# Hybrid mixer block on one core: a second Sx buffer, a third decay-matrix buffer, and two groups of instructions issued later

## The chip, the core and the metric

One core of a Trainium2 chip runs the whole program. The time is device microseconds from launch to end, median of several runs. The engines are PE (matrix products), DVE (vector), ACT (activations, casts and copies), POOL (here a DMA queue and some fills) and SP (a DMA queue).

## What is computed

One layer over 512 latent tokens of 1024 channels and 256 context tokens: a modulated RMSNorm, three mixers that run on the same input (a gated DeltaNet in both directions, a short gated convolution, a Fourier mixing), gates that merge them, an output projection, and a SwiGLU. All matrices are fp32. The change lies in the DeltaNet, which works on chunks of 64 tokens, four heads and two directions:

```python
g = jnp.cumsum(g, axis=-1)
decay = jnp.exp(jnp.where(lower, g[..., :, None] - g[..., None, :], -jnp.inf))
a = jnp.where(strict, jnp.einsum("bhnid,bhnjd->bhnij", kb, k) * decay, 0.0)
t_inv = lax.linalg.triangular_solve(a + eye, ...)      # unit lower triangular
u = t_inv @ (v * beta[..., None])
w = t_inv @ (kb * jnp.exp(g)[..., None])
attn = jnp.einsum("bhnid,bhnjd->bhnij", q, k) * decay
...
v_new = u_i - jnp.einsum("bhcd,bhde->bhce", w_i, s)    # scan over the chunks
o_i = jnp.einsum("bhcd,bhde->bhce", qg_i, s) + jnp.einsum("bhij,bhje->bhie", attn_i, v_new)
s = s * jnp.exp(gl_i)[..., None, None] + jnp.einsum("bhcd,bhce->bhde", kd_i, v_new)
```

## The kernel before, in words

**Main GEMMs.** `gemm_fm` multiplies a slice of 256 columns of a weight by the normalised input. Weights are fetched in halves of 512 KB by SP (`wf`, three buffers), split into a high part (an ACT cast, L143) and a low part (a DVE subtraction, L144), two buffers each, and multiplied three times (L255 to L257). A product with the 512 latent tokens (LAT) goes to a bank of pool `g` (three of them), one with the 256 context tokens (CTX) to a bank of pool `d` (four). In program order a half does first LAT, then CTX, with 24 instructions each.

**Order.** The program is written in Tile: each instruction has a priority (the places are, from the first to the last: setup, tri, sub, scan, prep, main), and within a place an earlier line goes first. A scheduler walks through the program with modelled times and gives each engine what is ready, by priority; on the chip each engine then runs its list in that fixed order, with semaphores. A buffer is asked for where the program makes the tile, and a tile with `bufs=1` waits until all readers of the one before it are done.

**DeltaNet.** Behind the key GEMM, at place `tri`, L404 to L440 work out the log decays G from the 16 columns of beta and alpha; L444 transposes them, DVE cumulates them (L447 to L466, giving `Gr`; scratch in `gtmp`, which has the tag `Sx`), and POOL stores `Gr` and a mirrored copy `Gn` to DRAM (L476 to L479). L480 to L502 turn them into columns: two transposes into a `d` bank (L481, L482), `Gc`, its exponentials `eGn` and `eG`, a product with ones into a second `d` bank (L494), the exponentials `eGl` and `ekd`, and the sigmoid of beta (L502). Then, at place `main`, come two value GEMMs (L504, LAT and CTX), each followed by its convolution and SiLU (`pairs`), and two query GEMMs.

For each of three batches of four chunk pairs (context, then two of latent tokens): `decay_gram` loads rows of decays from DRAM into `E` (L564, POOL), subtracts them from `Gc` (L565), takes exponentials, multiplies by Gram products (L578, in the single bank `t`) and scales; `substitute` inverts the 32x32 diagonal blocks by 60 dependent DVE steps (L611, L612) and stores them transposed to DRAM (L614); `inverse` loads them back (L620, `Sx`), transposes on DVE (L622), copies them to the diagonal of `TBD` (L625, four ACT copies), and makes the off-diagonal block: 64 products of 32x32 in bank `t` (L631; the trace's x64), two ACT copies to `Z` (L634), 64 products with `Sx` (L638), two ACT copies to `TBD` (L641). `scan(b)` does four dependent steps on `TBD` (L716). For the latent batches it first makes two masked decay matrices `ET` (L549 to L555: POOL load, two DVE steps, one exponential) at place `main`; each is read by two steps (L682). The order of calls is gram 0, gram 1, substitute both, inverse 0, scan 0, inverse 1, gram 2, substitute 2, scan 1, inverse 2, scan 2. Main GEMMs of later stages (L758 on) run on PE beside all this wherever they are ready.

Of the kernel before, what the change touches and what calls it, by code (L numbers as in the profile page):

```python
# [9 lines left out]
F32 = mybir.dt.float32  # L10
# [64 lines left out]
def body(tc, I, out):  # L75
    nc = tc.nc
    V, A, T, SY, GP = nc.vector, nc.scalar, nc.tensor, nc.sync, nc.gpsimd
    es = ExitStack()
    with es:
# [10 lines left out]
        pD = dstack.enter_context(tc.tile_pool(name="pD", bufs=1))  # L90
# [14 lines left out]
        def tbank(name="t"):  # L105
            return pst.tile([128, 512], F32, name=name, tag="t")

        def dbank(name="d"):
            return psd.tile([128, 512], F32, name=name, tag="d")
# [8 lines left out]
        def cst(name, rows=slice(None)):  # L118
            a, b = COFF[name]
            return cp[rows, a:b]  # L120
# [15 lines left out]
        def load_w(src, n=256):  # L136
            with prio("prep"):
                w = stg.tile([128, 4, 256], F32, name="wf", tag="wf", bufs=3)
                SY.dma_start(out=w[:, :, :n], in_=src)
            return w  # L140
# [5 lines left out]
        def prep_w(w, n=256, scale=None, dst=None):  # L146
            with prio("prep"):
                if dst is None:
                    wh = stg.tile([128, 4, 256], F32R, name="wh", tag="wh", bufs=2)
                    wl = stg.tile([128, 4, 256], F32R, name="wl", tag="wl", bufs=2)  # L150
                else:
                    wh, wl = dst
                if scale is not None:
                    V.tensor_tensor(out=w, in0=w, in1=scale, op=ALU.mult)  # L154
                split(w[:, :, :n], wh[:, :, :n], wl[:, :, :n])
            return wh, wl
# [97 lines left out]
        def mm3(ps, lh, ll, rh, rl, start, stop):  # L254
            T.matmul(ps, lhsT=lh, rhs=rh, start=start, stop=False)  # L255
            T.matmul(ps, lhsT=lh, rhs=rl, start=False, stop=False)  # L256
            T.matmul(ps, lhsT=ll, rhs=rh, start=False, stop=stop)  # L257
# [78 lines left out]
        def gemm_fm(wsrc, targets, n=256, kt=8):  # L336

            nt, mw = max(1, n // 128), min(n, 128)
            ps = {(ti, q): targets[ti][3]() for ti in range(len(targets)) for q in range(nt)}
            for half in range(kt // 4):  # L340
                wh, wl = prep_w(load_w(wsrc[:, 4 * half:4 * half + 4, :], n), n)
                for ti, (rh, rl, nn, _) in enumerate(targets):
                    for q in range(nt):
                        cs = slice(128 * q, 128 * q + mw)
                        for kk in range(4):
                            k = 4 * half + kk
                            mm3(ps[ti, q][0:mw, :nn], wh[:, kk, cs], wl[:, kk, cs], rh(k), rl(k), k == 0, k == kt - 1)
            return [[ps[ti, q] for q in range(nt)] for ti in range(len(targets))]
# [19 lines left out]
        def taps(base, stride, ft):  # L368
            return [cols2[:, base + stride * k + ft:base + stride * k + ft + 1] for k in range(3)]
# [4 lines left out]
        def pairs(dsts, ps, n, row, tp):  # L374

            y = cvt()[:, :n]
            conv3(y, ps[:, :n], tp, row)
            for i, dst in enumerate(dsts):
                sl = slice(256 * i, 256 * i + 256)
                d = dst.rearrange("p (m c j) -> p m c j", m=2, j=64)  # L380
                v = lambda t: t.rearrange("p (m b j) -> p m b j", m=2, j=64)
                A.activation(out=d[:, :, 0::3, :], in_=v(y[:, sl]), func=AF.Silu)
                A.activation(out=d[:, :, 1:3, :], in_=v(y[:, ::-1][:, sl]), func=AF.Silu)
# [19 lines left out]
        with prio("tri"):  # L403
# [38 lines left out]

            pg = dbank()
            T.transpose(pg[0:64, 0:128], G.rearrange("p a m h -> p (a m h)"), ident)  # L444
            gtmp = pD.tile([64, 512], F32, name="gtmp", tag="Sx", bufs=1)
            gr = gtmp[:, 0:128]
            V.tensor_copy(gr, pg[0:64, 0:128])  # L447
            gw = gtmp[:, 128:256]
# [28 lines left out]
            for i in range(2):  # L477
                GP.dma_start(out=Gd[:, 1, :, 32 * i:32 * i + 32].rearrange("u r j -> r u j"), in_=Gr[:, :, 32 - 32 * i:64 - 32 * i])
            GP.dma_start(out=Gdn.rearrange("u r j -> r u j"), in_=Gn)  # L479
            pg = dbank()  # L480
            T.transpose(pg[:, 0:64], Grf, ident[0:64, 0:64])  # L481
            T.transpose(pg[:, 64:128], Gn.rearrange("r u j -> r (u j)"), ident[0:64, 0:64])  # L482
            Gc = col("Gc")
            V.tensor_copy(flat(Gc), pg[:, 0:64])
            eGn = col("eGn")
            A.activation(out=flat(eGn), in_=pg[:, 64:128], func=AF.Exp)
            eG = col("eG")
# [7 lines left out]
            eGl = const.tile([128, 2, 64], F32, name="eGl")  # L495
            A.activation(out=eGl.rearrange("p u c -> p (u c)"), in_=pl[:, 0:128], func=AF.Exp)
            ekd = col("ekd")
# [2 lines left out]
                V.tensor_tensor(out=flat(ekd)[us], in0=pl[us, 64 * u:64 * u + 64], in1=flat(Gc)[us], op=ALU.subtract)  # L500
            A.activation(out=ekd, in_=ekd, func=AF.Exp)
            A.activation(out=bv, in_=bv, func=AF.Sigmoid)  # L502
        for g2 in range(2):
            pl_, pc_ = gemm_fm(win[:, :, 1024 + 256 * g2:1280 + 256 * g2], (LAT, CTX))  # L504
            for q in range(2):
                h = 2 * g2 + q
                tp = taps(0, 12, 8 + h)
                pairs([VT[0][:, h]], pc_[q], 256, 256, tp)
                pairs([VT[1][:, h], VT[2][:, h]], pl_[q], 512, 64, tp)
# [21 lines left out]
        TBD = pD.tile([128, 2, 16, 128], F32, name="TBD", tag="TBD")  # L531
# [14 lines left out]

        def decay_T(b, mm):

            ET = pD.tile([128, 2, 4, 64], F32, name="ET", tag="ET2", bufs=2)  # L549
            for u in range(2):  # L550
                src = Gdn[u].rearrange("(a r) j -> a r j", a=2)[:, 8 * b + 4 * mm:8 * b + 4 * mm + 4, :]
                GP.dma_start(out=ET[64 * u:64 * u + 64].rearrange("p a h j -> p a (h j)"), in_=src.rearrange("a r j -> a (r j)").partition_broadcast(64))
            V.tensor_tensor(out=ET, in0=ET, in1=Gc[:, :, 2 * b + mm, :].unsqueeze(3).broadcast_to([128, 2, 4, 64]), op=ALU.subtract)
            V.tensor_tensor(out=ET, in0=ET, in1=cst("mT").rearrange("p (a j) -> p a j", a=2).unsqueeze(2).broadcast_to([128, 2, 4, 64]), op=ALU.min)
            A.activation(out=ET, in_=ET, func=AF.Exp)  # L555
            return ET

# [58 lines left out]
        def inverse(b):  # L616

            slot, E = b % 2, Es[b]
            Sx = pD.tile([128, 16, 32], F32, name="Sx", tag="Sx", bufs=1)
            SY.dma_start(out=Sx, in_=Lt[b].rearrange("x p c -> p x c"))  # L620
            Sy = E[:, :, 0:32]
            V.transpose(out=Sy, in_=Sx)  # L622
            for q in range(4):
                qs = slice(32 * q, 32 * q + 32)
                A.copy(out=TBD[qs, slot, :, 32 * q:32 * q + 32], in_=Sy[qs])  # L625
            Z = pD.tile([128, 16, 32], F32, name="Z", tag="sh", bufs=1)
            bank = tbank()
            for i in range(16):
                for u in range(2):
                    a0, b0 = 64 * u, 64 * u + 32  # L630
                    T.matmul(bank[a0:a0 + 32, 32 * i:32 * i + 32], lhsT=E[b0:b0 + 32, i, 32:64], rhs=Sy[b0:b0 + 32, i, :],  # L631
                             start=True, stop=True, tile_position=(b0, a0))
            for a0 in (0, 64):
                A.copy(out=Z[a0:a0 + 32].rearrange("p i j -> p (i j)"), in_=bank[a0:a0 + 32])  # L634
            bank = tbank()
            for i in range(16):
                for a0 in (0, 64):
                    T.matmul(bank[a0:a0 + 32, 32 * i:32 * i + 32], lhsT=Sx[a0:a0 + 32, i, :], rhs=Z[a0:a0 + 32, i, :],  # L638
                             start=True, stop=True, tile_position=(a0, a0))
            for a0 in (0, 64):  # L640
                A.activation(out=TBD[a0:a0 + 32, slot, :, a0 + 32:a0 + 64], in_=bank[a0:a0 + 32].rearrange("p (i j) -> p i j", j=32),  # L641
                             func=AF.Copy)
# [11 lines left out]

        def scan_step(s, ET=None):
            b, par, m = s // 4, s % 2, s // 2
# [79 lines left out]
        def scan(b):  # L736
            ETs = [decay_T(b, mm) if b else None for mm in range(2)]
            with prio("scan"):
                for mm in range(2):
                    for par in range(2):  # L740
                        scan_step(4 * b + 2 * mm + par, ETs[mm])

        with prio("tri"):
            decay_gram(0)
            decay_gram(1)
            substitute((0, 1))
            inverse(0)
        scan(0)
        with prio("tri"):
            inverse(1)  # L750
            decay_gram(2)
            substitute((2,))
        scan(1)
        with prio("tri"):
            inverse(2)
# [351 lines left out]
```

## Time and profile before

| | |
|---|---|
| time, median of 3 runs | 975.82 us (973.52, 975.82, 976.12) |
| time of the profiled execution | 972.6 us |
| its span, first to last instruction | 970.8 us |
| PE busy | 953.0 us, 98% of the span |
| weight loads into PE (PEld) | 784.9 us, 81% |
| DVE busy | 544.4 us, 56% |
| ACT busy | 417.9 us, 43% |
| POOL busy | 28.8 us, 3% |
| mean granted PE clock | 0.997 of full speed |

In a timeline each row is a start (us from the start of the span), a duration, the engine, line, operation and the tiles written and read; in brackets the idle time of the engine before it, and what ended that. A row with a count (x64) is that many instructions merged.

### The profile page before, as it was taken

To read this page: it belongs to the slowest core of one execution; us is meant where nothing else is said; L and a number is where in the kernel's file an instruction comes from. 1 tells how busy PE (TensorE), PEld (TensorE's weight loads), DVE (VectorE), ACT (ScalarE), POOL (GpSimd) and SP (SyncE) were. 2 spreads that over 40 slices of the span, in tenths; PEclk is the share of its full clock that TensorE was granted. 3 is DMA by queue.
4 is the path that set the end of the run, shared out by engine and by line. 5 is a ranking of instruction groups with operands and counts; after the bars stand their busy time and mean duration, and the time that the engine had idled before them with its cause. 6 is when DMAs were issued, how large, how long until landed. Compare 5 with 4: busy or idle time off the path is not lost.

```text
span 970.8 us, 14622 instructions
## 1 busy us (share of the span) xinstructions
PE 953.0 (98%) x5964; PEld 784.9 (81%) x5964; DVE 544.4 (56%) x880; ACT 417.9 (43%) x729; POOL 28.8 (3%) x47
## 2 busy tenths in 40 slices
PE   8999999899999999999999999999999999999997
PEld 7587887778788888888878888988888888888885
DVE  3575888369765423788874977333333333434455
ACT  5363884687863334362234346332323232211224
POOL 1002200000000000000000000000000000000000
PEclk9999999999999999999999999999999999999999
DMA  9820542512202232837774352223233333232322
GB/s 336 285 66 4 133 131 83 136 45 55 57 23 65 87 109 69 306 110 270 252 237 158 103 173 62 69 87 105 92 100 95 95 102 89 91 103 89 106 87 87
DMA packets 96836, 115.30 MB, mean 119 GB/s; under 512 B 18124, under 2 KB 84032, under 8 KB 96768
## 3 DMA queue, kind: packets, MB, share of 16 engines
q1 hardware_dynamic: 88192, 109.01, 35.5%
q0 software_dynamic: 1632, 3.44, 1.7%
q10 hardware_dynamic: 6944, 1.91, 0.8%
q8 instruction: 47, 0.77, 0.3%
q14 instruction: 21, 0.17, 0.1%
HBM read 110.58 MB, written 3.77 MB: 118 GB/s over the span
## 4 chain that ended last, share of the span: by engine, by line
PE 45%; DMA 3%; DVE 2%; issue 0%; ACT 0%; DVEq 0%
PE g L257 12%; PE g L256 12%; PE g L255 11%; PE d L257 2%; PE d L256 2%; PE d L255 2%; DMA wf<-in_w_ffn_out_dram 2%; DVE wl L144 1%; PE t L257 1%; PE t L256 1%; PE t L255 1%; DMA wm<-in_w_mod_dram 1%; DMA wf<-in_w_gate_dram 1%; DVE wf L154 1%; PE d L1032 0%
## 5 line engine op out<-in xcount | busy, mean ns | idle before, releaser
L144 DVE TENSOR_TENSOR wl<-wf,wh 128x1024 fp32r<-128x1024 f32 x131 | 160.0, 1222 | 214.4 <-ACT wh L143 213.7
L143 ACT CAST wh<-wf 128x1024 fp32r<-128x1024 f32 x131 | 137.8, 1053 | 299.1 <-PE g L256 161.5
L257 PE MATMUL g<-hh,wl 128*128 128x512 f32 x368 | 146.2, 397 | 0.3 <-DVE wl L144 0.3
L256 PE MATMUL g<-hl,wh 128*128 128x512 f32 x368 | 146.0, 397 | 0.0
L255 PE MATMUL g<-hh,wh 128*128 128x512 f32 x368 | 145.8, 396 | 0.0
L255 PE MATMUL g<-h2h,wh 128*128 128x512 f32 (+1 forms) x352 | 133.6, 380 | 0.0
L257 PE MATMUL g<-h2h,wl 128*128 128x512 f32 (+1 forms) x352 | 133.5, 380 | 0.0
L256 PE MATMUL g<-h2l,wh 128*128 128x512 f32 (+1 forms) x352 | 133.5, 379 | 0.0
L257 PEld LDWEIGHTS g<-hh,wl 128*128 128x128 f32 x368 | 69.6, 189 | 14.3 <-DVE wl L144 0.7
L256 PEld LDWEIGHTS g<-hl,wh 128*128 128x128 f32 x368 | 69.6, 189 | 14.1 <-issue 0.5
L255 PEld LDWEIGHTS g<-hh,wh 128*128 128x128 f32 x368 | 69.5, 189 | 13.6 <-issue 0.2
L256 PEld LDWEIGHTS g<-h2l,wh 128*128 128x128 f32 x352 | 66.2, 188 | 12.6
L255 PEld LDWEIGHTS g<-h2h,wh 128*128 128x128 f32 x352 | 66.2, 188 | 12.5
L257 PEld LDWEIGHTS g<-h2h,wl 128*128 128x128 f32 x352 | 66.1, 188 | 12.4
L154 DVE TENSOR_TENSOR wf<-wf,g2b 128x1024 f32<-128x1024 f32 x22 | 27.0, 1225 | 55.1 <-DMA wf<-in_w_ffn_out_dram 55.0
L830 DVE SCALAR_TENSOR_TENSOR acc<-wm,ct,acc 128x1024 f32<-128x1024 f32 x32 | 41.0, 1282 | 15.5 <-DMA acc<-in_b_mod_dram 7.3
L256 PE MATMUL d<-wl,Ga 128*128 128x512 f32 x72 | 28.0, 390 | 0.0
L257 PE MATMUL d<-wh,Ga 128*128 128x512 f32 x72 | 28.0, 389 | 0.0
L255 PE MATMUL d<-wh,Ga 128*128 128x512 f32 x72 | 28.0, 389 | 0.0
L713 ACT ACTIVATE SJ<-SJ,eGl 128x128 f32<-128x128 f32 x80 | 25.2, 403 | 3.9 <-PE d L701 3.5
L143 ACT CAST Ga<-cvg 128x512 fp32r<-128x512 f32 x18 | 11.1, 619 | 25.4 <-DVE cvg L1078 25.4
L256 PE MATMUL g<-wl,Ga 128*128 128x512 f32 x54 | 21.2, 393 | 0.1
(464 smaller groups left out, 1704.9 us busy)
## 6 DMA issues: line engine op xcount, KB each, us to landing
wm<-in_w_mod_dram SPq DMA_DIRECT2D x48, 512.0 KB, 5.5
wf<-in_w_ffn_in_dram SPq DMA_DIRECT2D x44, 512.0 KB, 3.5
wf<-in_w_in_dram SPq DMA_DIRECT2D x31, 512.0 KB, 3.9
wf<-in_w_gate_dram SPq DMA_DIRECT2D x24, 512.0 KB, 3.7
wf<-in_w_ffn_out_dram SPq DMA_DIRECT2D x22, 512.0 KB, 3.5
wf<-in_w_o_dram SPq DMA_DIRECT2D x8, 512.0 KB, 3.6
xl<-in_x_dram SPq DMA_DIRECT2D x4, 512.0 KB, 5.3
wf<-in_w_sc_out_dram SPq DMA_DIRECT2D x4, 512.0 KB, 3.3
```

The costliest lines, as they stand in the source:

```text
L143: A.copy(out=hi, in_=f)
L144: V.tensor_tensor(out=lo, in0=f, in1=hi.bitcast(F32), op=ALU.subtract)
L154: V.tensor_tensor(out=w, in0=w, in1=scale, op=ALU.mult)
L255: T.matmul(ps, lhsT=lh, rhs=rh, start=start, stop=False)
L256: T.matmul(ps, lhsT=lh, rhs=rl, start=False, stop=False)
L257: T.matmul(ps, lhsT=ll, rhs=rh, start=False, stop=stop)
L713: A.activation(out=S[:, u ^ par, h], in_=S[:, u ^ par, h], func=AF.Copy, scale=eGl[:, u, c_:c_ + 1])
L830: V.scalar_tensor_tensor(out=acc, in0=w, scalar=ct[:, k, 0:1], in1=acc, op0=ALU.mult, op1=ALU.add)
```

## The change

`gtmp` and the `Sx` tiles get two buffers instead of one, `ET` three instead of two. The decay columns become a function that is called behind the first value GEMM, at place `main` instead of `tri`. In `inverse`, the four copies to the diagonal of `TBD` stand behind the two `Z` copies.

```diff
-            gtmp = pD.tile([64, 512], F32, name="gtmp", tag="Sx", bufs=1)
+            gtmp = pD.tile([64, 512], F32, name="gtmp", tag="Sx", bufs=2)
...
             GP.dma_start(out=Gdn.rearrange("u r j -> r u j"), in_=Gn)
+        def decay_columns():
             pg = dbank()
             T.transpose(pg[:, 0:64], Grf, ident[0:64, 0:64])
...
             A.activation(out=bv, in_=bv, func=AF.Sigmoid)
+            return Gc, eGn, eG, eGl, ekd
+
         for g2 in range(2):
             pl_, pc_ = gemm_fm(win[:, :, 1024 + 256 * g2:1280 + 256 * g2], (LAT, CTX))
+            if g2 == 0:
+                Gc, eGn, eG, eGl, ekd = decay_columns()
             for q in range(2):
...
-            ET = pD.tile([128, 2, 4, 64], F32, name="ET", tag="ET2", bufs=2)
+            ET = pD.tile([128, 2, 4, 64], F32, name="ET", tag="ET2", bufs=3)
...
-            Sx = pD.tile([128, 16, 32], F32, name="Sx", tag="Sx", bufs=1)
+            Sx = pD.tile([128, 16, 32], F32, name="Sx", tag="Sx", bufs=2)
             SY.dma_start(out=Sx, in_=Lt[b].rearrange("x p c -> p x c"))
             Sy = E[:, :, 0:32]
             V.transpose(out=Sy, in_=Sx)
-            for q in range(4):
-                qs = slice(32 * q, 32 * q + 32)
-                A.copy(out=TBD[qs, slot, :, 32 * q:32 * q + 32], in_=Sy[qs])
...
             for a0 in (0, 64):
                 A.copy(out=Z[a0:a0 + 32].rearrange("p i j -> p (i j)"), in_=bank[a0:a0 + 32])
+            for q in range(4):
+                qs = slice(32 * q, 32 * q + 32)
+                A.copy(out=TBD[qs, slot, :, 32 * q:32 * q + 32], in_=Sy[qs])
             bank = tbank()
```

## Rows read from the trace of the kernel before

**Rows 1.** The page's head and busy times of the engines.

```profile
span 970.8 us, 14622 instructions
PE 953.0 (98%) x5964; PEld 784.9 (81%) x5964; DVE 544.4 (56%) x880; ACT 417.9 (43%) x729; POOL 28.8 (3%) x47
```

**Rows 2.** Windows: busy time and count by engine, granted clock, DMA share, GB/s.

```profile
84.00:87.00 3.00, 3.00 (x18) 2.27 (x9) 1.40 (x7) 1.53 (x3) 0.00 (x0) 0.50 0.00 0
...
93.00:96.00 3.00, 1.66 (x9) 0.95 (x8) 2.12 (x12) 0.64 (x3) 1.61 (x3) 1.00 0.04 11
...
178.00:204.00 26.00, 22.85 (x490) 18.09 (x490) 8.81 (x16) 21.72 (x42) 2.12 (x4) 1.00 0.29 73
...
700.00:800.00 100.00, 100.00 (x443) 82.82 (x442) 34.30 (x37) 29.36 (x37) 0.00 (x0) 1.00 0.32 100
```

The engines of a window stand in the order PE, PEld, DVE, ACT, POOL.

**Rows 3.** Timeline of PE around the decay columns, and four transposes later.

```profile
92.70 0.39 PE L256 MATMUL g<-hl,wh 128*128 128x512 f32 x1
92.93 0.39 PE L257 MATMUL g<-hh,wl 128*128 128x512 f32 x1
94.15 0.27 PE L481 MATMUL d<-cp,Gr 64*128 64x64 f32 x1 [0.83 <-DVE Gr L465]
...
95.62 0.39 PE L255 MATMUL d<-HC,wh 128*128 128x256 f32 x1
...
101.47 0.40 PE L255 MATMUL g<-hh,wh 128*128 128x512 f32 x1
...
213.45 0.66 PE L664 MATMUL d<-cp,KV 128*128 128x128 f32 x4
```

**Rows 4.** Timelines of ACT and DVE around the decay columns.

```profile
83.76 0.24 ACT L502 ACTIVATE beta<-beta 128x48 f32<-128x48 f32 x1 [2.74 <-DVE beta L424]
...
85.73 0.19 DVE L429 TENSOR_SCALAR smt<-smt 128x48 f32<-128x48 f32 x1 [1.43 <-ACT smt L428]
...
105.15 1.22 DVE L565 TENSOR_TENSOR E<-Gc,E 128x1024 f32<-128x1024 f32 x1
```

**Rows 5.** Timeline of PE: the blocks of the three inverses.

```profile
178.74 1.20 PE L631 MATMUL t<-E 32*32 32x32 f32 x64 [0.34 <-issue]
...
182.47 1.20 PE L638 MATMUL t<-Z,Sx 32*32 32x32 f32 x64 [0.46 <-ACT Z L634]
...
188.94 1.20 PE L631 MATMUL t<-E 32*32 32x32 f32 x64 [0.89 <-issue]
...
192.60 1.20 PE L638 MATMUL t<-Z,Sx 32*32 32x32 f32 x64 [0.80 <-ACT Z L634]
...
263.83 1.20 PE L638 MATMUL t<-Z,Sx 32*32 32x32 f32 x64 [0.39 <-ACT Z L634]
```

**Rows 6.** Timeline of ACT in the first inverse.

```profile
178.73 2.50 ACT L625 COPY TBD<-E 32x512 f32<-32x512 f32 x4 [2.40 <-DVE E L622]
181.25 1.16 ACT L634 COPY Z<-t 32x512 f32<-32x512 f32 x2
...
183.71 1.19 ACT L641 ACTIVATE TBD<-t 32x512 f32<-32x512 f32 x2 [0.69 <-PE t L638]
```

**Rows 7.** Sx: SP's second load in the timeline, and landing times of all three.

```profile
183.71 0.37 SPq L620 DMA_DIRECT2D Sx<-Lt  x1
...
DMA to landing us min/median/max: 3.5/4.4/4.7
```

**Rows 8.** Timelines of POOL, DVE and PE around the ETs of scan 2.

```profile
236.72 1.18 POOL L552 DMA_DIRECT2D ET<-Gdn  x2 [53.08 <-DVE ATb L682]
...
241.53 0.69 DVE L553 TENSOR_TENSOR ET<-ET,Gc 128x512 f32<-128x512 f32 x1 [1.42 <-DMA ET<-Gdn]
...
263.11 0.69 DVE L553 TENSOR_TENSOR ET<-ET,Gc 128x512 f32<-128x512 f32 x1 [3.04 <-DMA ET<-Gdn]
...
244.92 0.66 PE L669 MATMUL d<-cp,KV 128*128 128x128 f32 x4 [1.47 <-DVE SJ L729]
```

**Rows 9.** The waits: total us, times, longest.

```profile
POOL E L564 <- ACT TBD L625: 76.3, 1, 76.3
```

## The prediction

> **What bounds the kernel now.** I read the page first, for the span and the busy shares; then the windows, to see in which stretches PE idles; then the timelines of PE, ACT, DVE, SP and POOL in those stretches; last the waits of the tiles that the change touches (Sx, ET, TBD, E).
>
> PE is busy 98% of the span and no other engine comes near it [rows 1]. In a stretch of the later weight stages it is busy every microsecond, while ACT and DVE are busy about a third of the time [rows 2]. So the kernel is bound by PE, and a change that gives PE no less work can win only what PE loses today to waits. Those losses lie in three places that the change touches. From 93 to 96 us PE is busy 1.66 of 3.00 us [rows 2]: it has done the latent half of the first value GEMM and stands at L481, which waits for DVE's cumulated decays (Gr) [rows 3]. From 178 to 204 us, where the inverses of batches 0 and 1 lie, PE is busy 22.85 of 26 us, and ACT 21.72 [rows 2]; the waits stand at L631 and L638 [rows 5]. At 244.92 PE waits 1.47 us for a DVE update of the state that is itself queued behind a wait for an ET load [rows 8]. Outside these, the scan may end sooner or later without moving the end, since main matmuls fill PE anyway.
>
> **Decay columns (L480 to L502), issued after the first value GEMM.** The stretch from the start of the last main matmul before it to the first one after it is 95.62 - 92.93 = 2.69 us [rows 3]. It holds one main matmul, 0.23 us by the step from 92.70 to 92.93, and four small PE instructions; four transposes of 128 columns took 0.66 us elsewhere, which I take for these four. 2.69 - 0.23 - 0.66 = 1.80 us of loss. After the change 48 main matmuls with 256 columns, which now start at 95.62, stand ahead of L481 in program order, and they need nothing of the decays; so Gr is long ready when PE comes to it. The bounds are the idle time alone, 3.00 - 1.66 = 1.34, and 2.46 if the small matmuls cost nothing between main ones. I take 1.80.
> Why PE did not run those 48 first today is not in a row; I take it from the code: their two banks are asked for after the two banks of the decay columns, from a pool of four. The move reverses that. If the banks were not the reason, this term falls to near 0 (the second rival).
> The moved block issues no DMA: its four POOL transfers stay where they were, and SP has none. Its five activations and few DVE steps come some 3 to 5 us later. Who waits: L565 of the first Gram stage, which needs Gc and starts at 105.15 [rows 4], against a new Gc at about 95.62 - 1.80 + 48 x 0.12 = 99.6 (48 matmuls take 5.85 us between 95.62 and 101.47). Cover of 5 us; if it went, the substitution would start later, and main matmuls would fill PE. The sigmoid L502 ran at 83.76, ahead of the first exponential of the softplus chain, and DVE waited 1.43 us for that exponential [rows 4]; moved back it may leave that chain, at no gain, since PE no longer waits for the chain. Gr shares its buffer with the substitution's products, which the program reaches only behind two Gram stages: nothing.
>
> **Second Sx buffer.** Today batch 1's load is issued at 183.71, just after the L638 block of batch 0 that reads the only buffer, and such a load lands in 3.5 to 4.7 us [rows 5, 7]. L631 of batch 1 then finds PE idle for 0.89 us [rows 5]. With two buffers both loads go out together near 173 us, behind the same store of the substitution, and no weight load queues behind a blocked load on SP. Gain 0.89, bounds 0 (another wait ends last, the single t bank) and 0.89. I take 0.9. The first inverse's own 0.34 stays: its load is no earlier.
>
> **Diagonal copies after Z.** ACT runs four copies (2.50 us) and then the two Z copies (1.16) before L638 can start [rows 6]; L638 waits 0.46, 0.80 and, in batch 2, 0.39 us, 1.65 together [rows 5]. Lines do not set the order on an engine by themselves: L502 ran 10 us ahead of L481 [rows 3, 4], so an engine is given what is ready. The diagonal copies are ready when the transpose is; Z only when the 1.20 us block L631 is done. So about two of the four copies still go ahead, and 1.25 us leaves the chain in each inverse. That exceeds each wait, but PE's order is planned anew for the shorter chain, and a planned order misses again. I take half, 0.8; bounds 0 and 1.65. What is late next: the L641 copies, behind the two remaining diagonal copies, beside L638. The E buffer of batch 0 comes free up to 2.5 us later, and POOL's load for batch 2 waits for exactly that copy [rows 9]; that delays the last substitution at most as much, and main matmuls cover it.
>
> **Third ET buffer.** Scan 2 uses two ETs, and one buffer is added. The first can load near 105 us; the second still waits for a buffer of scan 1, which comes free at the same step, and its load is issued at about the same 236.7 as today's first [rows 8]. DVE would again stand in front of it (1.42 us), with the state update queued behind. What goes is the other wait, 3.04 us at 263.11, behind which PE lost nothing that rows show. Gain 0; bounds 0 and 1.47.
> The Trainium skill (Trainium Kernel Development and Optimization, Best Practices) says to double-buffer so that transfers lie beside work. By that rule the wait at 244.92 goes as well and the sum grows by 1.47 us; the rows of this stretch speak for one load helped and one not.
>
> **Sum.** 1.80 + 0.9 + 0.8 + 0 = 3.5 us. The profiled execution took 972.6 us (span 970.8 and 1.8 around it), so 969.1 against it. It lies 0.9 us below the fastest of the three runs shown and 3.2 below their median; I put the difference on the median: 975.8 - 3.5 = 972.3.
>
> **Rivals.**
> First, PE starves in the inverses. With both Sx loaded, the two inverses can be planned back to back, and each hands its single t bank to ACT and back: Z copies 1.16, L641 copies 1.19 [rows 6]. Without main matmuls between, PE idles 2.35 us per inverse, and 2.50 more where the four diagonal copies still go first. ACT is busy 21.72 of 26 us there [rows 2], and its weight casts feed those main matmuls, which speaks for it; against it, after both L631 and L638 of batch 0 main matmuls were ready and ran. Price: 4.7 to 9.7 us of idle in place of today's 0.34 + 0.46 + 0.89 + 0.80 = 2.49, less the 1.80 of the columns: 0.4 to 5.4 slower. It decides for slower once the idle time of the two passes 2.49 + 1.80 = 4.3 us. Taken at 3.2 slower, 979.0.
> Second, the move does not do what it says: the columns or the copies keep their place on the engines, or waits of the same size come back where the new plan misjudges a load. Then only 0.9 to 1.8 of the terms is left: 974.5.
> Third, all of it: the columns at 2.46, the copies at 1.65, Sx 0.89 and ET 1.47 make 6.5, 969.3.
> Fourth, the clock. From 84 to 87 us, after a run of small matmuls, the granted clock was 0.50, the 1.2 GHz level, which cost half of 3.00 us, 1.5; through 178 to 204 it was 1.00 in spite of 256 small ones [rows 2]. Two inverses in a row could bring one such drop each: 3.0 of the 3.5 is given back, 975.3.
> The Trainium skill (TensorE: Matmul & The Clock Gate, Why this matters for your kernels) tells that idle gaps between matmul bursts bring the clock down to half. By that rule the idle 93 to 96 us should be a place for a drop, and the granted clock stayed at 1.00 there [rows 2]; so I give this rival little.
>
> **How the numbers follow.** Forecast 45%, between 970.8 and 973.8 by the halves of its terms; first rival 12%, second 25%, third 12%, fourth 6%. 0.3% is 2.9 us, about what a measurement of this kernel can tell from no change; the bound is 972.9. Of the forecast's 45%, 38 lie beyond it and 7 short of it. Faster: 38 + 12 = 50%. Same: 7 + 25 + 5 of the clock = 37%. Slower: 12 + 1 = 13%. The range goes from 967.5 (the third rival, less the spread of the runs of some 2 us) to 978.0 (the second rival and the mild end of the first, with the same spread).
>
> **What would show it.** Right: main matmuls run on through 93 to 96 us, with L481 behind the 256-column ones; two Sx loads within 1 us near 173; Z copies with at most two diagonal copies ahead; L638's waits under 0.3; one ET load near 105 and one near 237, with the DVE wait still there. Wrong: PE idle at a new place before 110 us, or more than 4.3 us of PE idle between 178 and 204; a granted clock of 0.50 in the inverses; or the ET wait gone.

## The result, and the profile after

The changed kernel takes 970.85 us (median of 10 runs, 968.6 to 973.03), beside 975.97 for the kernel before (10 runs, 972.12 to 980.62): a ratio of 0.9946, interval 0.9925 to 0.9967. Forecast was 972.3. The profiled executions differ by less: 969.97 against 972.6 us.

The page's head and busy times after, against [rows 1]:

```profile
span 968.2 us, 14628 instructions
PE 952.9 (98%) x5964; PEld 785.1 (81%) x5964; DVE 543.2 (56%) x880; ACT 421.8 (44%) x733; POOL 28.8 (3%) x47
```

PE does the same work in a span 2.6 us shorter, so what went is waiting. The windows of [rows 2] say where; the engines stand in the same order:

```profile
84.00:87.00 3.00, 3.00 (x15) 2.39 (x8) 1.40 (x7) 1.53 (x2) 0.00 (x0) 0.50 0.00 0
93.00:96.00 3.00, 3.00 (x24) 2.87 (x23) 1.98 (x11) 0.80 (x1) 1.60 (x3) 1.00 0.04 11
178.00:204.00 26.00, 24.81 (x506) 19.88 (x505) 10.60 (x18) 22.51 (x44) 2.11 (x4) 1.00 0.29 75
700.00:800.00 100.00, 100.00 (x443) 82.81 (x442) 36.54 (x39) 29.82 (x38) 0.00 (x0) 1.00 0.31 95
```

From 93 to 96 us PE is busy throughout (1.66 of 3.00 before); in the two inverses it idles 26 - 24.81 = 1.19 us in place of 3.15. The timeline of PE after, at the moved columns:

```profile
95.12 0.40 PE L257 MATMUL g<-hh,wl 128*128 128x512 f32 x1
...
96.05 0.28 PE L255 MATMUL d<-HC,wh 128*128 128x256 f32 x1
...
99.00 0.27 PE L482 MATMUL d<-cp,Gr 64*128 64x64 f32 x1
99.11 0.22 PE L483 MATMUL d<-cp,gtmp 64*128 64x64 f32 x1
99.18 0.44 PE L495 MATMUL d<-gtmp,ones 64*128 64x128 f32 x2
99.54 0.50 PE L255 MATMUL g<-hh,wh 128*128 128x512 f32 x1
```

The 48 context matmuls now stand ahead of the first decay transpose (L482, L481 before), which waits for nothing, and the next latent product starts at 99.54 in place of 101.47 [rows 3].

To follow a gain along the span I take the start of the n-th main matmul (L255 to L257) before, less its start after, and call it the lead. It is 1.76 to 1.83 us from 126 to 176 us, 2.86 at 340, when the DeltaNet is over, and 2.4 to 3.0 at the end. So the traced gain is 1.8 us from the columns and about 1.0 from the inverses and scans.

PE in the first two inverses after, against [rows 5] (L633 was L631, L643 was L638):

```profile
179.49 1.20 PE L633 MATMUL t<-E 32*32 32x32 f32 x64 [0.19 <-issue]
...
183.67 0.31 PE L643 MATMUL t<-Z,Sx 32*32 32x32 f32 x7 [0.26 <-issue]
...
186.05 1.20 PE L633 MATMUL t<-E 32*32 32x32 f32 x64
...
188.96 1.20 PE L643 MATMUL t<-Z,Sx 32*32 32x32 f32 x64 [0.16 <-ACT Z L636]
191.45 1.10 PE L583 MATMUL t<-KV 128*32 128x64 f32 x64 [0.42 <-ACT TBD L646]
```

The second inverse's first block waits for nothing (0.89 us before), the Z blocks wait 0.26 and 0.16 (0.46 and 0.80), and the wait of the next Gram products for the L646 copies is 0.42 (0.21 before). SP issues both Sx loads ahead of both inverses, 1.85 us apart. ACT puts two of the four diagonal copies (L639) ahead of Z (L636) in the first inverse, but all four in the second: two of them are among the four copies at 182.28, two stand at 186.02. In the third inverse three go ahead. SP, then ACT, after, against [rows 6, 7]:

```profile
175.56 0.38 SPq L625 DMA_DIRECT2D Sx<-Lt  x1
...
177.41 0.45 SPq L625 DMA_DIRECT2D Sx<-Lt  x1
```

```profile
179.84 1.24 ACT L639 COPY TBD<-E 32x512 f32<-32x512 f32 x2
181.09 1.17 ACT L636 COPY Z<-t 32x512 f32<-32x512 f32 x2
182.28 2.51 ACT L639 COPY TBD<-E 32x512 f32<-32x512 f32 x4
...
186.02 1.24 ACT L639 COPY TBD<-E 32x512 f32<-32x512 f32 x2
...
187.75 1.16 ACT L636 COPY Z<-t 32x512 f32<-32x512 f32 x2
```

The ETs of the second latent scan, on POOL, DVE and PE after, against [rows 8]:

```profile
233.74 1.18 POOL L557 DMA_DIRECT2D ET<-Gdn  x2 [47.82 <-DVE ATb L687]
...
238.60 0.69 DVE L558 TENSOR_TENSOR ET<-ET,Gc 128x512 f32<-128x512 f32 x1 [1.43 <-DMA ET<-Gdn]
...
242.03 0.66 PE L674 MATMUL d<-cp,KV 128*128 128x128 f32 x4 [1.33 <-DVE SJ L734]
```

One ET is still late, and PE waits 1.33 us behind it (1.47 before).

The traces account for 2.6 to 2.9 us; the medians differ by 5.1. Part of the rest goes with PE's granted clock, whose mean is given for every timed execution. Over 93 executions of the kernel before (those timed beside the experiments) it is 0.9946 on average. The 44 at 0.994 or less have a median of 977.07 us, the 31 at 0.997 or more one of 972.96. Over the changed kernel's ten it is 0.9967, and one shows 0.994 or less. One less the mean clock, times the span, is the time given up to the lower clock: 5.3 us before, 3.2 after. Not all of it is lost: within the kernels, an execution that gave up 1 us more by this measure took 0.68 us longer (235 executions, standard error 0.04). So the difference of 2.1 us is worth an estimated 1.4 of the medians, at most 2.1. The profiled execution of before had 0.997, so neither its trace nor the prediction shows this part.

### The profile page after: what moved, and what is told of

The parts are those of the page before. It is cut to its first block, busy times and chain, and to the rows that moved or that the text cites. A ratio compares the mean times of both kernels' runs of the same rounds, so it can differ in the third digit from the quotient of the medians.

```text
span 968.2 us, 14628 instructions
## 1 busy us (share of the span) xinstructions
PE 952.9 (98%) x5964; PEld 785.1 (81%) x5964; DVE 543.2 (56%) x880; ACT 421.8 (44%) x733; POOL 28.8 (3%) x47
## 4 chain that ended last, share of the span: by engine, by line
PE 83%; DVE 6%; ACT 5%; DMA 4%; issue 2%; POOL 0%; SPq 0%; DVEq 0%; ACTq 0%
PE g L256 19%; PE g L257 19%; PE g L255 19%; PE d L255 5%; PE d L256 5%; PE d L257 5%; DMA wm<-in_w_mod_dram 2%; DVE acc L835 1%; DVE wl L144 1%; PE t L257 1%; PE t L255 1%; PE t L256 1%; PE d L238 1%; ACT TBD L639 1%; DMA acc<-in_b_mod_dram 1%
## 5 line engine op out<-in xcount | busy, mean ns | idle before, releaser
L144 DVE TENSOR_TENSOR wl<-wf,wh 128x1024 fp32r<-128x1024 f32 x131 | 160.1, 1222 | 205.0 <-ACT wh L143 204.1
L257 PE MATMUL g<-hh,wl 128*128 128x512 f32 x368 | 146.0, 397 | 0.3 <-DVE wl L144 0.3
L255 PE MATMUL g<-hh,wh 128*128 128x512 f32 x368 | 146.1, 397 | 0.0
L255 PE MATMUL g<-h2h,wh 128*128 128x512 f32 (+1 forms) x352 | 133.6, 380 | 0.0
L257 PE MATMUL g<-h2h,wl 128*128 128x512 f32 (+1 forms) x352 | 133.5, 380 | 0.0
L257 PEld LDWEIGHTS g<-hh,wl 128*128 128x128 f32 x368 | 69.6, 189 | 15.0 <-DVE wl L144 1.0
L255 PEld LDWEIGHTS g<-hh,wh 128*128 128x128 f32 x368 | 69.6, 189 | 13.6 <-issue 0.2
L255 PEld LDWEIGHTS g<-h2h,wh 128*128 128x128 f32 x352 | 66.2, 188 | 12.6
L257 PEld LDWEIGHTS g<-h2h,wl 128*128 128x128 f32 x352 | 66.1, 188 | 12.3
L255 PE MATMUL d<-wh,Ga 128*128 128x512 f32 x72 | 28.0, 389 | 0.0
L257 PE MATMUL d<-wh,Ga 128*128 128x512 f32 x72 | 28.0, 389 | 0.0
L616 DVE TENSOR_TENSOR t<-W 128x30 f32<-128x30 f32 (+29 forms) x60 | 19.3, 322 | 3.7 <-issue 2.7
```

Of the source, the lines that this page charges most:

```text
L144: V.tensor_tensor(out=lo, in0=f, in1=hi.bitcast(F32), op=ALU.subtract)
L616: V.tensor_tensor(out=t, in0=W3[0:n, j + 1:, j:j + 1].broadcast_to(sh_), in1=W3[0:n, j:j + 1, 0:j].broadcast_to(sh_), op=ALU.mult)
```

## The experiments

Twelve kernels ran, in three sets of four (1 to 4, 5 to 8, 9 to 12), each set beside the kernel before, whose medians were 974.58, 974.76 and 975.51 us. Each ratio is against the kernel before of its own set, so medians of different sets compare only to about 1 us. "Less clock" in the table is the mean over the executions of the time less (1 - clock) x span, with its standard error: what the kernel would take without the lower clock if all of that time were lost. By the 0.68 above it takes off too much, an estimated 3 to 4 us for the four kernels at 0.9913 or less and 1 to 2 for the others.

| kernel | median us (range, runs) | ratio, interval | mean clock | at 0.994 or less | less clock, us |
|---|---|---|---|---|---|
| before | 975.06 (970.62 to 980.11, 93) | | 0.9946 | 44 of 93 | 970.0 ± 0.2 |
| changed | 970.85 (968.6 to 973.03, 10) | 0.9946, 0.9925 to 0.9967 | 0.9967 | 1 of 10 | 967.6 ± 0.4 |
| 1 columns | 980.05 (975.28 to 984.13, 12) | 1.0057, 1.0036 to 1.0077 | 0.9902 | 11 of 12 | 970.0 ± 0.5 |
| 2 all but columns | 971.91 (970.53 to 973.09, 12) | 0.9971, 0.9954 to 0.9987 | 0.9969 | 0 of 12 | 968.9 ± 0.3 |
| 3 changed, ET apart | 970.64 (968.3 to 973.07, 12) | 0.9958, 0.9941 to 0.9974 | 0.9968 | 0 of 12 | 967.5 ± 0.4 |
| 4 columns in old place, no new banks | 981.52 (978.39 to 983.48, 6) | 1.0073, 1.0048 to 1.0098 | 0.9882 | 6 of 6 | 969.8 ± 0.5 |
| 5 columns, Sx | 971.99 (969.06 to 974.79, 12) | 0.9966, 0.9948 to 0.9984 | 0.9960 | 2 of 12 | 967.7 ± 0.3 |
| 6 all but Sx | 972.34 (969.75 to 977.98, 12) | 0.9973, 0.9955 to 0.9992 | 0.9967 | 2 of 12 | 969.6 ± 0.3 |
| 7 Sx | 971.41 (969.09 to 973.15, 12) | 0.9958, 0.9941 to 0.9974 | 0.9972 | 1 of 12 | 968.6 ± 0.3 |
| 8 copies | 975.34 (971.94 to 979.68, 12) | 0.9998, 0.9974 to 1.0022 | 0.9947 | 5 of 12 | 970.3 ± 0.5 |
| 9 ET | 975.50 (970.82 to 977.72, 12) | 0.9999, 0.9980 to 1.0019 | 0.9942 | 7 of 12 | 969.5 ± 0.5 |
| 10 columns, ET | 977.41 (975.05 to 979.62, 12) | 1.0010, 0.9994 to 1.0026 | 0.9913 | 12 of 12 | 969.1 ± 0.4 |
| 11 columns, copies | 980.15 (976.94 to 983.18, 11) | 1.0051, 1.0032 to 1.0069 | 0.9904 | 11 of 11 | 970.7 ± 0.5 |
| 12 columns, Sx, ET apart | 968.66 (965.66 to 972.77, 7) | 0.9931, 0.9906 to 0.9956 | 0.9971 | 1 of 7 | 966.5 ± 0.7 |

### 1. The columns alone

```diff
+        def decay_columns():
             pg = dbank()
...
+            if g2 == 0:
+                Gc, eGn, eG, eGl, ekd = decay_columns()
```

> The kernel before with the decay columns alone moved behind the first value GEMM. Theory (PE lost 1.8 us there because the columns' two banks were asked for ahead of the GEMM's): PE has no idle time from 93 to 96 us, the second value GEMM starts 1.9 us earlier, the first gate sigmoid starts near 326.6 instead of 328.4, and the time falls by 1.5 to 2.2 us, a ratio of about 0.998. Rival (most of the measured 5 us comes from here, a wait that the one profiled execution shows too small): ratio 0.996 or less. Rival (the loss comes back later): first gate sigmoid at 328.

980.05 us: slower than before, by 0.6%. Yet the lead is 1.84 us up to 176 us, as in the changed kernel; the term is right where it arises. It is lost in the inverses. The windows there:

```profile
188.00:192.00 4.00, 1.82 (x44) 1.29 (x44) 1.29 (x2) 0.73 (x2) 0.00 (x0) 1.00 0.34 57
192.00:196.00 4.00, 4.00 (x89) 3.48 (x85) 1.84 (x2) 3.92 (x8) 0.00 (x0) 0.65 0.00 0
264.00:268.00 4.00, 2.47 (x19) 1.71 (x18) 1.38 (x2) 1.99 (x7) 0.00 (x0) 1.00 0.76 108
268.00:272.00 4.00, 2.63 (x69) 2.34 (x69) 0.71 (x1) 3.17 (x6) 0.00 (x0) 0.54 0.01 1
```

And the timelines of PE and DVE:

```profile
191.52 1.20 PE L636 MATMUL t<-E 32*32 32x32 f32 x64 [2.18 <-issue]
...
269.37 1.92 PE L636 MATMUL t<-E 32*32 32x32 f32 x64 [2.91 <-DVE E L627]
...
190.71 0.71 DVE L627 STREAM_TRANSPOSE E<-Sx 128x512 f32<-128x512 f32 x1 [9.53 <-DMA Sx<-Lt]
...
266.49 0.69 DVE L558 TENSOR_TENSOR ET<-ET,Gc 128x512 f32<-128x512 f32 x1 [4.14 <-DMA ET<-Gdn]
```

With the single Sx buffer SP issued the second load at 185.09, and its transpose began 5.6 us later (4.4 before, from 183.71 [rows 7] to 188.13). PE waited 2.18 us at the second inverse, and in the next window the granted clock was 0.65, at the 1.2 GHz level for most of it. In the third inverse DVE stood 4.14 us in front of an ET, the transpose behind it in its queue, PE waited 2.91 us, and the clock fell again. The lead is -5.25 at 340 us. Another 3.0 us go between 400 and 500 us, outside all that the change touches: PE waits 1.61 us at 476.32 for a DVE split (L144), and from 476 to 480 us the clock is 0.57.

The Trainium skill (TensorE: Matmul & The Clock Gate, HAM oscillation — how this bites in real kernels) describes this: PE, waiting between bursts for a transfer that brings the next operand, finds itself at half clock when it resumes. The third inverse agrees with it. In the second the clock fell only after PE had resumed at 191.52 (1.00 up to 192, 0.65 behind), and experiments 6 and 11 show that it does not happen each time.

### 2. All but the columns

The change without the hunk of experiment 1.

> The changed kernel with the decay columns back in their old place, so second Sx buffer, third ET buffer and later copies alone. Theory: the 1.8 us at 93 to 96 us are back, the waits in the inverses are small as in the changed kernel, 0.5 to 1.7 us faster than before, ratio 0.998 to 1.000; first gate sigmoid near 327.4. Rival (the inverses carry most of the gain): ratio 0.997 or less and first gate sigmoid near 326.

971.91 us, a lead of 0.88 at 340 us, of which 0.37 stood at 176 us, ahead of the inverses. So the remaining three parts have about 0.5 in this trace, and the clock of 0.997. The columns are worth about 1.1 us of the medians in the changed kernel (971.91 - 970.85), 1.3 "less clock" and 2.4 by the ratios; the intervals of the ratios overlap, so that they gain there at all is not shown by the times alone.

### 3. The second ET of the last scan in another tag

```diff
-            ET = pD.tile([128, 2, 4, 64], F32, name="ET", tag="ET2", bufs=3)
+            ET = pD.tile([128, 2, 4, 64], F32, name="ET", tag="Sx" if (b, mm) == (2, 1) else "ET2", bufs=2 if (b, mm) == (2, 1) else 3)
```

> The changed kernel, but the second ET of scan 2 uses a buffer of the tag Sx, which is free from the second inverse on, instead of waiting for one of scan 1. Theory (the DVE wait for this load and PE's wait behind it are what the third buffer left over): the load goes out near 190 us instead of 234, the 1.43 us DVE wait at 238.6 and PE's wait of about 1.3 us behind it go, and the kernel gains 1.0 to 1.6 us on the changed one; ratio to before about 0.993. Rival (the wait is covered, or another one takes its place within a few us): same time as the changed kernel within 0.4 us by the first gate sigmoid (325.6).

970.64 us, no difference from the changed kernel. The wait itself is gone. POOL, then PE:

```profile
191.31 1.18 POOL L557 DMA_DIRECT2D ET<-Gdn  x2 [5.15 <-PE t L643]
...
242.27 0.69 PE L683 MATMUL d<-qT,KV 128*64 128x64 f32 x16 [0.22 <-DVE SJ L734]
```

The load goes out 42 us earlier, PE waits 0.12 and 0.22 in place of 1.33, and from 235 to 245 us it is busy 9.65 us in place of 8.67. But the two waits at the start of the first inverse are 0.57 and 0.89 (0.19 and 0.26 in the changed kernel); the lead is 1.61 at 176 us and 3.20 at 340, against 1.82 and 2.86. So of the 1.0 us won at PE about half was given back; that the new layout of the engines' lists did it is argued, not shown.

### 4. The columns in their old place, in a bank that is already held

```diff
-            pg = dbank()
+            pg = pbt[:, 128:256]
...
-            pl = dbank()
+            pl = pbt[:, 256:384]
```

> The kernel before, columns in their old place, but written to free columns of the bank that held beta and alpha, so that they ask for no bank of their own. Theory (banks, not the place in the program, held back the 48 context matmuls): these run from 92 us on, beside L481, L482 and L494; PE idles less than 0.4 us from 93 to 96 us; first gate sigmoid near 326.8; ratio about 0.998, like the columns alone. Rival (the place in the program does it): PE still idles over 1 us there, time as before.

This tests why PE did not run ahead before. PE around the columns:

```profile
92.65 0.36 PE L255 MATMUL d<-HC,wh 128*128 128x256 f32 x1
...
94.64 0.27 PE L481 MATMUL d<-cp,Gr 64*128 64x64 f32 x1
94.85 0.39 PE L257 MATMUL d<-HC,wl 128*128 128x256 f32 x1
```

The context matmuls start at 92.65, before the decays are cumulated, in place of 95.62 [rows 3]: the banks were what held them. Yet the lead, which was -0.5 at 90 us, is only 0.4 at 126 and 0.8 at 160. The small matmuls now come one by one between main ones, and each takes a longer step: from 94.29 over L481 to 94.85, where the steps between main matmuls are 0.12. So a free bank wins about half of the term (0.9 us from 90 to 126); that the rest comes from the small matmuls standing side by side behind the GEMM fits these steps, but was not tried by itself. In the inverses it lost as experiment 1 did (a wait of 2.54 us at the second), at a mean clock of 0.988.

### 5. Columns and the second Sx buffer

Experiment 1 with `bufs=2` in the tag `Sx` (both lines of the change's diff).

> The kernel before with two parts of the change: the columns moved, and two Sx buffers; the copies and the ET buffers stay. Theory (the moved columns alone brought the drops of the granted clock because the single Sx buffer held the second and third inverse up for 2 to 3 us; with a second buffer this goes): the waits of PE at the block that reads E in the second and third inverse are under 1 us, the mean granted clock is back at 0.996 to 0.997 from 0.990, no half-clock interval between 185 and 280 us, and the median is 971.0 to 973.0 us, 7 to 9 us below that of the columns alone. Rival (the drops come from the order of the scan that follows the earlier Gram stages, whatever Sx does, and it is the later copies or the third ET that keep them away in the whole change): clock 0.990, 978 to 981 us.

971.99 us at 0.996, 8 us below the columns alone, and no window of the trace from 184 to 280 us has a clock under 1.00. PE's waits at the E blocks of the first two inverses are 0.70 and 0.59. One size, in two lines, turns 0.6% slower into 0.3% faster.

### 6. The changed kernel with one Sx buffer

```diff
-            Sx = pD.tile([128, 16, 32], F32, name="Sx", tag="Sx", bufs=2)
+            Sx = pD.tile([128, 16, 32], F32, name="Sx", tag="Sx", bufs=1)
```

(and the same for `gtmp`).

> The changed kernel with one Sx buffer again; columns, copies and ET as changed. Theory (the single Sx buffer is what makes the moved columns lose): a wait of 1.5 us or more at the block that reads E in the second inverse, half-clock intervals between 185 and 280 us, a mean granted clock of 0.990 to 0.992 and 977 to 981 us. Rival (copies or ET keep the clock up): clock 0.996 to 0.997, 970.5 to 973 us, so that the Sx buffer is worth its own wait of 0.9 us alone.

Both were half right. The profiled execution (977.98 us) shows the theory's wait and its drop, in the windows and in PE's timeline:

```profile
188.00:192.00 4.00, 1.21 (x41) 1.05 (x40) 1.29 (x2) 0.54 (x1) 0.00 (x0) 1.00 0.25 59
192.00:196.00 4.00, 4.00 (x68) 3.38 (x64) 1.76 (x2) 3.92 (x8) 0.00 (x0) 0.57 0.00 0
```

```profile
191.53 1.25 PE L633 MATMUL t<-E 32*32 32x32 f32 x64 [2.79 <-issue]
```

But the other eleven executions lie between 969.75 and 974.4, with a mean clock of 0.997: the rival's numbers. None of the eleven has a trace, so whether they had the wait is not shown; the theory's lower clock and time they did not have. "Less clock" the second buffer is worth 969.6 - 967.6 = 2.0 us here.

### 7. The second Sx buffer alone

The two `bufs=2` lines in the kernel before.

> The kernel before with two Sx buffers and nothing else. By the prediction's term: the 0.89 us wait of the second inverse goes, main matmuls lead by 0.9 us at 340 us, 973.7 us against a before of 974.6. If the single buffer also feeds the clock drops of the kernel before (mean granted clock 0.995 over its executions against 0.997 of the variants with two buffers): 1.5 us more, 972 us, and 0.9965 or more. Rival (another wait ends last in the second inverse): no lead, 974 to 975 us.

971.41 us, 0.9958: from one size in two lines comes most of what the whole change gives, and the second expectation was nearest. The mean clock is 0.997, and one execution of twelve is at 0.994 or less. The lead of 2.74 us at 340 holds 1.49 that is chance: from 84 to 87 us this execution kept the full clock, where the profiled one of before had 0.50 [rows 2]. The rest, 1.25, arises in the inverses and scans: the two waits of the second inverse give 0.75 of it (0.89 and 0.80 before, 0.71 and 0.23 now). That window, and PE in the second inverse:

```profile
84.00:87.00 3.00, 3.00 (x24) 2.41 (x15) 1.40 (x7) 1.57 (x3) 0.00 (x0) 1.00 0.00 0
```

```profile
184.77 1.20 PE L631 MATMUL t<-E 32*32 32x32 f32 x64 [0.71 <-ACT TBD L641]
...
187.99 1.20 PE L638 MATMUL t<-Z,Sx 32*32 32x32 f32 x64 [0.23 <-ACT Z L634]
```

The inverses lie closer together, the second 4.2 us earlier (1.4 of it the lead already there). Its first block no longer waits for the load but for ACT's L641 copies, the case that the prediction gave as this term's lower bound.

### 8. The later copies alone

```diff
-            for q in range(4):
-                A.copy(out=TBD[...], in_=Sy[qs])
...
+            for q in range(4):
+                A.copy(out=TBD[...], in_=Sy[qs])
             bank = tbank()
```

> The kernel before with the diagonal copies issued behind the Z copies and nothing else. By the prediction's term: the 0.46, 0.80 and 0.39 us waits of PE at the block that reads Z shrink by half, 0.8 us lead at 340 us, and the clock as before (0.995): about 973.8 us. Rival (the Z copies still wait for two diagonal copies and PE's new order spends the gain): a lead of 0 to 0.3 us, 974.3 to 974.9 us. Against both: a clock of 0.997 would say that the shorter inverses take away the drops, 972 us.

975.34 us, 0.9998, the clock as before. Every engine's list has the same instructions in the same order as in the kernel before, apart from line numbers: without the other parts the scheduler still puts all four diagonal copies ahead of Z. So this is the kernel before a second time, and a measure of how well two sets of runs agree.

### 9. The third ET buffer alone

```diff
-            ET = pD.tile([128, 2, 4, 64], F32, name="ET", tag="ET2", bufs=2)
+            ET = pD.tile([128, 2, 4, 64], F32, name="ET", tag="ET2", bufs=3)
```

> The kernel before with a third ET buffer and nothing else. If the ET wait ahead of the third inverse (3.04 us of DVE at 263.11 in the kernel before) is what brings half-clock intervals in part of its executions: that wait is gone, the mean granted clock over the executions is 0.9965 or more against 0.995 of before, and the median is 972 to 973.2 us. Rival (those intervals come from the single Sx buffer in the second inverse, or from elsewhere): the wait is gone too, the clock stays at 0.995, 974 to 975.3 us, which is the prediction's nothing.

975.50 us, 0.9999, clock 0.994: the rival, and the prediction's nothing. DVE's wait at 263.11 is gone, the one near 240 stays (1.42 us of DVE at 239.64).

### 10 and 11. Columns with ET, columns with copies

Experiment 1 with the edit of experiment 9, then with that of experiment 8.

> The columns moved and a third ET buffer; one Sx buffer, the copies in their old place. The columns alone took 980.05 us at a clock of 0.990, and with copies and ET both 972.34 at 0.997. If it is the third ET buffer that keeps the clock up (no ET wait ahead of the third inverse, PE busy through it): 0.996 to 0.997, 971.5 to 973 us, and PE still waits 2 us or more at the block that reads E in the second inverse. If it is the copies: 0.990, 978 to 981 us.

> The columns moved and the diagonal copies issued later; one Sx buffer, two ET buffers. The mirror of the run with the third ET buffer: if the copies keep the clock up, 0.996 to 0.997 and 971.5 to 973 us; if the ET buffer does, 0.990 and 978 to 981 us with a wait of 2.5 us or more of PE in the third inverse, behind DVE's wait for ET; if either does in part, between the two.

977.41 us at 0.9913 and 980.15 at 0.9904: neither part by itself keeps the clock up beside the moved columns, against the first expectation of each. ET helps (1.0010 against 1.0057 for the columns alone, and the intervals do not meet). PE waits 1.19 us at its third inverse, 2.91 in experiment 1, though the clock fell there too: 0.50 from 272 to 275 us. In the other the drop is in the third inverse, behind DVE's 4.54 us for an ET. Windows of columns and copies there:

```profile
260.00:264.00 4.00, 2.94 (x22) 2.11 (x21) 0.67 (x1) 1.58 (x5) 0.00 (x0) 1.00 0.85 120
264.00:268.00 4.00, 2.57 (x66) 2.29 (x67) 1.91 (x4) 3.07 (x6) 0.00 (x0) 0.62 0.01 2
```

Its second inverse also held PE up (2.02 us at L633), and no drop followed that one.

Both parts together, beside the columns and one Sx buffer, are experiment 6: 0.9973. Adding ET to columns and copies thus won 0.8%, adding the copies to columns and ET 0.4%, with intervals that do not meet in either case. What each part is worth depends on the others.

### 12. Columns, Sx and ET apart, the copies in their old place

The edits of experiments 1, 5 and 3.

> The changed kernel with the copies in their old place and the second ET of the last scan in the tag of Sx. If the copies gave nothing of their own (the kernel with the copies alone had every engine in the order of before, and the second Sx buffer alone was as fast as Sx, copies and ET together): 970 to 971 us, level with the changed kernel and with the variant that only sets ET apart. If the copies do carry 0.8 us in this company: 971.3 to 972 us.

968.66 us, 0.9931: faster than the kernel before, and the lowest median of all, but its interval overlaps that of the changed kernel, so it is not shown to beat it. That it is slower without the later copies does not show. In its trace PE waits 0.17 us at 241.63, where the changed kernel waits 1.33.

## Why the prediction was right, and where it was not

**Decay columns, 1.80.** Right in place, cause and size: the lead of 1.76 to 1.84 in two kernels, and experiment 4 for the banks. What reaches the end depends on what follows: 1.1 us of the medians in the changed kernel, nothing that can be told from noise in company of Sx alone (971.99 against 971.41, intervals that overlap), and 5 us lost alone. "Outside these, the scan may end sooner or later without moving the end" was the step that failed here: with one Sx buffer the inverses, come to earlier, starved PE.

**Second Sx buffer, 0.9.** The mechanism is right in the changed kernel, where the 0.89 us wait went. Alone, the wait for the load went too, but one of 0.71 for the L641 copies stood in its place; the traced gain of 1.25 lies near the term and comes largely from elsewhere. The term was mis-sized as a whole: 975.06 - 971.41 = 3.6 us between the medians. The time given up to the lower clock fell from 5.3 to 2.8 us, worth an estimated 1.7 at 0.68 each; that part this step did not look at.

**Diagonal copies, 0.8.** Wrong. Alone they change no engine's order. That two copies go behind Z came true only with the other parts, and in the changed kernel in the first inverse alone; in the second all four still go ahead. With two Sx buffers no gain shows, "less clock": 968.6 for Sx alone and 968.9 for Sx, copies and ET, 967.7 and 967.6 with the columns. With one Sx buffer, the columns and ET they did pay (experiments 10 and 6), by a path that no term describes. "An engine is given what is ready" was not enough to say what the scheduler would do.

**Third ET buffer, 0.** Right, alone (0.9999) and in its mechanism: one load helped, one not. It is not nothing in all company: beside the moved columns and one Sx buffer the wait that it takes away stood in front of the third inverse (experiments 1, 10 and 11). The Trainium skill's advice to double-buffer (Trainium Kernel Development and Optimization, Best Practices), put beside this term in the prediction, holds for Sx and, alone, not for ET, where the wait that PE feels stayed.

**What else moved.** The sigmoid did not move back (83.72 on ACT after, 83.76 before), at no cost. Cover for the columns' consumers held: Gc is there after 99.75, and the first Gram stage reads it at 103.58. What the prediction did not count: the moved exponentials now stand between SiLUs on ACT, with two more table loads, 1.28 us each at 101.95 and 103.76; PE has no wait there.

**The sum.** 3.5 us forecast; 2.6 in the profiled executions, 5.1 in the medians. The step that failed is "I put the difference on the median": the profiled execution's 3.2 us below the median is not all noise that both kernels share, but in part a lower clock (0.994 or less) that the kernel before has in about half of its executions. The second Sx buffer alone leaves it in one of twelve. That 972.3 came so near 970.85 is therefore partly luck: the copies' 0.8 did not show, and 1.4 to 2.1 us of clock, which are in no term, took its place.

**The rivals.** The first was a real risk in another form: not back-to-back inverses, which ran with waits of up to 0.89 us (experiment 3), but a single Sx buffer starved PE. The second is true of the copies. The fourth had the sign reversed: two inverses in a row kept the clock, and waits before an inverse lost it. Its low chance leaned on one idle stretch that kept the clock, 93 to 96 us; that was no test, since the idle there came in three waits of 0.83 us or less, and the drops at the inverses of these runs followed single waits of 1.19 to 2.94 us.

**What stays open.** No trace of the kernel before shows one of its lower-clock executions, so that its drops lie in the second inverse is argued, from the kernels with two Sx buffers (5 of 65 executions at 0.994 or less, against 12 of 24 for copies or ET alone). Experiment 6 kept the clock in most executions with one Sx buffer; experiments 10 and 11 show that it needs both ET and the copies for that, but why is not settled. Of the 5.1 us between the medians, the trace and the clock together make 4.0 to 5.0; the rest is within the interval of the ratio.

## What to carry to other kernels

Where PE is the bound, compare the granted clock of all timed executions, not of the profiled one alone: here a wait of 2 to 3 us at PE often cost twice, once as idle time and once at half clock behind it. A part that is worth its price where it lies can lose it at the next transfer whose buffer is still in use, so try parts in pairs before dropping one. Check on the engines' lists that a move in the program moved anything.

## What the runs showed of the hardware that was not expected

The same list of instructions does not always get the same clock: the stretch from 84 to 87 us had a granted clock of 0.50 in the profiled executions of the changed kernel and of the kernel before [rows 2], and 1.00 in those of experiments 7 and 12, PE being busy 3.00 of 3.00 us in all four, with PE's list the same up to there. After a wait of 2.79 us at the second inverse (experiment 6) the clock fell to the 1.2 GHz level. After 2.02 us (experiment 11) it stayed at 2.4 GHz, and so it did after the 0.89 us of before and the 1.34 idle of 93 to 96 us [rows 2, 5]; but after 1.19 us at the third inverse (experiment 10) it fell. The length of the last wait alone does not settle it. And one transfer took 4.4 us from issue to its reader in the kernel before, 5.6 to 6.4 in four kernels with moved columns and one Sx buffer, with the DMA engines 0.88 to 0.93 busy from 184 to 188 us (0.79 before); that the load waits for others there is argued, not tried.
